# Attention units issued two at a time in a hybrid attention and recurrence layer

## The chip, the cores and the metric

One core of one Trainium2 chip runs the whole kernel. The metric is device time in microseconds (us), the median of a few runs. The program's engines are TensorE (PE, with PEld for its weight loads), VectorE (DVE), ScalarE (ACT), GpSimd (POOL) and the DMA queues, of which SyncE (SP) issues nearly all.

## What is computed

One inference step of one layer over 2048 prompt rows and 32 sample rows. Eight heads do stick-breaking attention, eight heads a matrix-state recurrence, and a projection and a gated feed-forward follow. The part that the change touches is the attention of the prompt:

```python
z = einsum('bqhd,bkhd->bhqk', q, k) / sqrt(64)
mask = k_pos < q_pos
log_1mb = where(mask, log_sigmoid(-z), 0)
after = reverse_cumsum(log_1mb) - log_1mb
weight = where(mask, exp(log_sigmoid(z) + after), 0)
o = einsum('bhqk,bkhd->bqhd', weight, v)
...
x = x + concat(attention, recurrence) @ w_out
x = x + (silu(h2 @ w_gate) * (h2 @ w_up)) @ w_down
```

## The kernel before

The kernel has three stages one after the other: the input projection (to about 940 us of the profile), the middle stage, and the output projection with the feed-forward. The middle stage is the one at issue. It has three generators, which one loop (L1165 to L1173) advances by turns, always the one with the least issued work for its size: `attention()` (L924), `recurrence()` (L997), which walks 33 chunks of 64 rows and each time goes from PE to DVE or ACT and back five times, and `first_rows()` (L1142), which does a part of the output projection.

`attention()` walks head by head through blocks of 512 queries (qg) and of 512 keys (kc), from the newest keys to the oldest. A block has four score units and four turn units. 

- A score unit, `scores` (L818), takes 128 queries: two matmuls (L824, L825, the high and the low part of an fp32 split) into a tile z in PSUM, on a diagonal block a third (L827) that adds the mask, then `stick` (L774): ACT makes the sigmoid R of z (L776) and DVE runs a multiplying scan over R, backwards (L778), which also reads z. Pool psZ has 3 buffers for z.
- A turn unit, `turn` (L832), takes 128 keys: up to four transposes (L837) of pieces of R into a tile wt in PSUM, then `split` (L103): ACT casts wt to wth (L104), and DVE subtracts wth from wt to get wtl (L105). Pool psW has 2 buffers for wt, so the transposes of a turn wait for the subtraction of the turn before the last.
- A values unit, `values` (L844), multiplies wth and wtl with the value rows (L851, L852) and sums in one PSUM tile (psO).

There are 320 units of each kind for the prompt, plus 6 for the sample rows (`s_scores`, `s_turn`, `s_values`). The main loop of `attention()` (L945 to L962) takes one unit of each per round: score unit t, then a turn whose last score lies LAG = 4 back, then the values of turns that are LAG2 = 2 rounds old. After that it yields to the other generators, with the work of the round as its weight. A list scheduler then orders the instructions of each engine, mostly as they were issued, and lets one go ahead of another that it takes to be waiting. Transposes (L837, L875, L990) and the recurrence's matmuls run on plain fp32; scores, values and the output projection (L760) on the one-pass type fp32r.

Of the kernel before, what the change touches and what calls it, by code (L numbers as in the profile page):

```python
# [52 lines left out]
def kernel(ctx: ExitStack, tc: tile.TileContext, x_prompt, x_sample, cache_k, cache_v,  # L53
# [709 lines left out]
    with tc.tile_pool(reuse_waits="tile", name="bp", bufs=6) as bp, \  # L763
# [8 lines left out]
        NB, LAG, LAG2, LOOK, RW = 12, 4, 2, 8, PAST + TS + 1  # L772
# [45 lines left out]
        def scores(h, qg, kc, j):  # L818

            k = pieces[h, kc][0]  # L820
            n = (j + 1) * P if kc == qg else 512
            z = psZ.tile([P, 512], F32, tag="z", name="z")
            js = slice(j * P, (j + 1) * P)
            PE.matmul(z[:, 0:n], state[h, qg][:, 0, js], k[:, 0:n], start=True, stop=False)  # L824
            PE.matmul(z[:, 0:n], state[h, qg][:, 1, js], k[:, 0:n], start=False, stop=kc != qg)  # L825
            if kc == qg:
                PE.matmul(z[:, n - P:n], identr, mnegr, start=False, stop=True)  # L827
            R = bk.tile([P, 512], F32, tag="R", name="R", bufs=NB)
            stick(z, R, n, 1.0 if kc == qg else state[h, qg, kc + 1, j][:, 0:1])
            state[h, qg, kc, j] = R  # L830

        def turn(h, qg, kc, kb):  # L832

            j0 = kb if kc == qg else 0
            pt = psW.tile([P, 512], F32, tag="wt", name="wt")
            for j in range(j0, 4):
                PE.transpose(pt[:, j * P:(j + 1) * P], state[h, qg, kc, j][:, kb * P:(kb + 1) * P], ident)  # L837
            wh = bq.tile([P, 512], F32R, tag="wth", name="wth", bufs=4)
            wl = bq.tile([P, 512], F32R, tag="wtl", name="wtl", bufs=4)
            c0 = j0 * P  # L840
            split(wh[:, c0:], wl[:, c0:], pt[:, c0:])
            state[h, qg, kc, "w", kb] = (wh, wl)
# [19 lines left out]
        def s_scores(kc, e):  # L862
            n = TS if kc == 2 else 512
            if kc == 2:
                R = bs.tile([P, RW], F32, tag="Rs", name="Rs")
                POOL.memset(R[:, PAST + TS:PAST + TS + 1], 1.0)
                state["R", e] = R
            elif e == 0:
                ck = bs.tile([P, TP], F32, tag="ck", name="ck").rearrange("p (j n) -> p j n", j=4)
                kT = bs.tile([P, TP], F32, tag="kT", name="kT").rearrange("p (c k) -> p c k", c=4)  # L870
                SP.dma_start(ck, cache_k[0, 0, kc * 512:(kc + 1) * 512].rearrange("(j p) h d -> p j (h d)", p=P))
                for c in range(4):
                    pt = psW.tile([P, 512], F32, tag="wt", name="ckt")
                    for j in range(4):
                        PE.transpose(pt[:, j * P:(j + 1) * P], ck[:, j, c * P:(c + 1) * P], ident)  # L875
                    (ACT.copy if c % 2 else DVE.tensor_copy)(kT[:, c, :], pt)
                SP.dma_start(ck, cache_v[0, 0, kc * 512:(kc + 1) * 512].rearrange("(j p) h d -> p j (h d)", p=P))
                state["ck", kc], state["kT", kc] = ck, kT
            z = psZ.tile([P, 512], F32, tag="z", name="zs")
            if kc == 2:  # L880
                PE.matmul(z[:, 0:n], ident, mnegs, start=True, stop=False)
            for c in range(4):
                rhs = kTs[64 * e:64 * e + 64, c, :] if kc == 2 else state["kT", kc][64 * e:64 * e + 64, c, :]
                PE.matmul(z[32 * c:32 * c + 32, 0:n], qTs[64 * e:64 * e + 64, c, :], rhs,
                          start=kc < 2, stop=True)
            b = bs.tile([P, 512], F32, tag="bs", name="bs", bufs=4)
            s_stick(z, state["R", e], b, kc * 512, n)
            state["b", kc, e] = b

        def s_turn(kc, e):  # L890
            n = TS if kc == 2 else 512
            pt = psW.tile([P, 512], F32, tag="wt", name="wts")
            for k0 in range(0, n, P):
                m = min(P, n)
                PE.transpose(pt[0:m, k0:k0 + P], state["b", kc, e][:, k0:k0 + m], ident)
            wT = bs.tile([P, 512], F32, tag="wTs", name="wTs")
            m = min(P, n)
            DVE.tensor_copy(wT[0:m, 0:max(n, P)], pt[0:m, 0:max(n, P)])
            state["w", kc, e] = wT

        def s_values(kc, e):
            n = TS if kc == 2 else 512
            if kc == 2 and e == 0:
                av = psO.tile([P, 512], F32, tag="av", name="avs")
                state["o"] = av
                PE.matmul(av[0:64, 0:H * TS], vTs[:, 0:HD], zr.to_broadcast([TS, H * TS]), start=True, stop=False)
            av, wT = state["o"], state["w", kc, e]
            for k0 in range(0, n, P):
                m = min(P, n)
                for c in range(4):  # L910
                    h = 2 * c + e
                    vv = vTs[:, h * HD:(h + 1) * HD] if kc == 2 else state["ck", kc][:, k0 // P, h * HD:(h + 1) * HD]
                    PE.matmul(av[0:64, h * TS:(h + 1) * TS], vv, wT[0:m, k0 + 32 * c:k0 + 32 * c + 32],
                              start=False, stop=kc == 0 and k0 == 384 and e == 1 and c == 3)
            if kc == 0 and e == 1:
                os_ = bq.tile([64, 512], F32, tag="oT", name="os", bufs=2)
                ACT.copy(os_[:, 0:256], av[0:64, 0:256])
                SP.dma_start(mixT_d[0:512, TP:TT].rearrange("(h d) q -> d h q", d=HD),
                             os_[:, 0:256].rearrange("d (h q) -> d h q", q=TS))
# [4 lines left out]
        def attention():  # L924
            A, B, loads = [], [], []
            for hq, h in [(hq, h) for hq in range(2) for h in range(H)]:
                if hq == 0 and h == 2:
                    for kc in (2, 1, 0):
                        for e in range(2):
                            A.append((lambda kc=kc, e=e: s_scores(kc, e), 1.0 if kc == 2 else 3.0))  # L930
                        for e in range(2):
                            B.append((len(A) - 1, lambda kc=kc, e=e: s_turn(kc, e),
                                      lambda kc=kc, e=e: s_values(kc, e), 0.2 if kc == 2 else 2.0))
                for qg in (2 * hq, 2 * hq + 1):
                    for kc in range(qg, -1, -1):
                        loads.append((len(A), h, qg, kc))
                        for j in range(4):
                            n = (j + 1) * P if kc == qg else 512
                            A.append((lambda h=h, qg=qg, kc=kc, j=j: scores(h, qg, kc, j), 2 * n / 2400))
                        for kb in range(4):  # L940
                            m = 4 - (kb if kc == qg else 0)
                            B.append((len(A) - 1, lambda h=h, qg=qg, kc=kc, kb=kb: turn(h, qg, kc, kb),
                                      lambda h=h, qg=qg, kc=kc, kb=kb: values(h, qg, kc, kb),
                                      m * (0.107 + 2 * P / 2400)))
            t, nb, pend = 0, 0, []  # L945
            while t < len(A) or nb < len(B) or pend:
                w = 0.0
                while loads and loads[0][0] <= t + LOOK:
                    load(*loads.pop(0)[1:])
                if t < len(A):  # L950
                    A[t][0]()
                    w += A[t][1]
                if nb < len(B) and (B[nb][0] <= t - LAG or t >= len(A)):
                    B[nb][1]()
                    pend.append((t, B[nb][2]))
                    w += B[nb][3]
                    nb += 1
                while pend and (pend[0][0] <= t - LAG2 or nb == len(B)):
                    pend.pop(0)[1]()
                    done["values"] += 1  # L960
                t += 1
                yield w  # L962

        def normalise(Yt, t0, n):

# [200 lines left out]
        while gens:  # L1166
            g = min(gens, key=lambda x: x[1] / x[2])
            with priority(tc, g[3]):
                w = next(g[0], None)
# [14 lines left out]
    with tc.tile_pool(reuse_waits="tile", name="c1", bufs=1) as cp, tc.tile_pool(reuse_waits="tile", name="psM", bufs=6, space=PSUM) as psM, \  # L1184
# [38 lines left out]
        with tc.tile_pool(reuse_waits="tile", name="co", bufs=2) as co:  # L1223
            gb = co.tile([P, D], F32, name="gb", bufs=1)
            SP.dma_start(gb, norm_ffn_g.to_broadcast([P, D]))
            wpool, w = done["w"]
            ws = wo_weights(co, 0, lambda: row2("wor"))
            w = next(ws), w
# [159 lines left out]
```

## Time and profile before

| | us |
|---|---|
| median of 3 runs | 3451.93 (3447.23 to 3460.93) |
| the profiled execution, its own time | 3450.89 |
| its span, first to last instruction | 3448.7 |
| PE busy in the span | 3273.3 (95%) |
| DVE busy in the span | 1763.8 (51%) |
| middle stage, first score to last values matmul | about 945 to 1785 |

The shares of busy time are means over three stages with different limits. The middle stage is the only one whose instructions move, so it has to be read by itself.

### The profile page before, as it was taken

What the parts mean: (1) busy time and instruction counts of PE and PEld (TensorE: products, weight loads), DVE (VectorE), ACT (ScalarE), POOL (GpSimd) and SP (SyncE); (2) the same over time, 40 slices, a digit from 0 to 9 for tenths busy, and PEclk for the clock granted to TensorE, in tenths of its full rate; (3) what the DMA queues carried; (4) which work ended last, traced back from release to release, by engine and by line L of the source; (5) the groups of instructions that cost most, each with busy time, mean ns of one, the idle gap of its engine ahead of it and who ended that gap; (6) DMA issues with size and microseconds to landing.
All of it is one profiled execution on the core that took longest, in us unless ns stands there. A gap on an engine that the chain in (4) does not pass through costs nothing.

```text
span 3448.7 us, 50501 instructions
## 1 busy us (share of the span) xinstructions
PE 3273.3 (95%) x20281; PEld 2830.4 (82%) x20281; DVE 1763.8 (51%) x2449; ACT 1159.5 (34%) x2231; POOL 856.4 (25%) x719
## 2 busy tenths in 40 slices
PE   8998898889699999999999999999999999999998
PEld 7988898878567777777777999999999888888887
DVE  4675757678679788887762322222222323212223
ACT  6434353434256455555542411111112311111111
POOL 3322423253101121122123421122112321222121
PEclk9999999989899899999999999999999999999999
DMA  5555564565765665656544511111111411111111
GB/s 149 162 157 153 174 175 137 172 181 153 209 178 149 157 152 156 171 143 159 158 106 128 192 50 45 42 50 43 43 49 56 166 49 42 50 43 49 49 43 49
DMA packets 481762, 395.82 MB, mean 115 GB/s; under 512 B 72228, under 2 KB 403568, under 8 KB 481528
## 3 DMA queue, kind: packets, MB, share of 16 engines
q1 hardware_dynamic: 393000, 346.58, 35.2%
q10 hardware_dynamic: 88528, 46.02, 5.0%
q8 instruction: 160, 2.62, 0.3%
q14 instruction: 74, 0.61, 0.1%
HBM read 278.19 MB, written 114.31 MB: 114 GB/s over the span
## 4 chain that ended last, share of the span: by engine, by line
PE 50%; DVE 1%; DMA 1%; issue 0%; ACT 0%; POOL 0%; SPq 0%; POOLq 0%; ACTq 0%
PE gu L1301 29%; PE dn L1321 15%; PE mo L760 3%; PE wt L837 0%; PE pt L1217 0%; DVE R L778 0%; PE av L851 0%; PE av L852 0%; DMA mx<-mixT_d 0%; PE z L825 0%; PE sap L1100 0%; PE yp L1122 0%; PE snp L1109 0%; PE yp L1124 0%; PE z L824 0%
## 5 line engine op out<-in xcount | busy, mean ns | idle before, releaser
L1324 DVE TENSOR_TENSOR x<-x,dn 128x512 f32<-128x512 f32 x374 | 255.7, 687 | 243.3 <-PE dn L1321 243.3
L778 DVE TENSOR_TENSOR_SCAN R<-R,z 128x512 f32<-128x512 f32 (+2 forms) x320 | 347.7, 1089 | 57.8 <-ACT R L776 55.0
L1301 PE MATMUL gu<-h2h,wh 128*128 128x352 f32 (+1 forms) x1760 | 368.3, 351 | 1.7 <-ACT wh L104 1.2
L1301 PE MATMUL gu<-h2h,wl 128*128 128x352 f32 (+1 forms) x1760 | 369.0, 351 | 0.0
L1301 PE MATMUL gu<-h2l,wh 128*128 128x352 f32 (+1 forms) x1760 | 367.3, 351 | 0.0
L1301 PEld LDWEIGHTS gu<-h2h,wh 128*128 128x128 f32 x1760 | 305.0, 188 | 33.9 <-ACT wh L104 1.4
L1301 PEld LDWEIGHTS gu<-h2l,wh 128*128 128x128 f32 x1760 | 305.3, 188 | 31.0
L1301 PEld LDWEIGHTS gu<-h2h,wl 128*128 128x128 f32 x1760 | 305.1, 188 | 30.2
L1321 PE MATMUL dn<-dh,hdh 128*128 128x512 f32 x748 | 295.1, 394 | 0.0
L1321 PE MATMUL dn<-dh,hdl 128*128 128x512 f32 x748 | 295.0, 394 | 0.0
L1321 PE MATMUL dn<-dl,hdh 128*128 128x512 f32 x748 | 293.8, 393 | 0.0
L324 PE MATMUL mm<-hh,wh 128*128 128x384 f32 (+4 forms) x1296 | 248.8, 334 | 2.7 <-ACT xp L336 1.2
L324 PE MATMUL mm<-hh,wl 128*128 128x384 f32 (+4 forms) x1296 | 235.6, 324 | 0.0
L324 PE MATMUL mm<-hl,wh 128*128 128x384 f32 (+4 forms) x1296 | 231.3, 320 | 0.0
L776 ACT ACTIVATE R<-z 128x512 f32<-128x512 f32 (+2 forms) x320 | 171.2, 537 | 151.0 <-PE z L825 82.5
L324 PEld LDWEIGHTS mm<-hh,wh 128*128 128x128 f32 (+1 forms) x1296 | 211.7, 193 | 9.8 <-ACT xp L336 1.6
L324 PEld LDWEIGHTS mm<-hh,wl 128*128 128x128 f32 (+1 forms) x1296 | 212.0, 191 | 2.6
L324 PEld LDWEIGHTS mm<-hl,wh 128*128 128x128 f32 (+1 forms) x1296 | 207.5, 187 | 2.6
L105 DVE TENSOR_TENSOR wtl<-wt,wth 128x512 fp32r<-128x512 f32 (+1 forms) x320 | 189.0, 591 | 27.0 <-ACT wth L104 25.5
L837 PE MATMUL wt<-ident,R 128*128 128x128 f32 x1088 | 186.2, 283 | 14.2 <-DVE wtl L105 13.6
L104 ACT CAST wth<-wt 128x512 fp32r<-128x512 f32 (+1 forms) x320 | 166.6, 521 | 80.7 <-PE wt L837 77.1
L104 ACT CAST dh<-rawd 128x1024 fp32r<-128x1024 f32 x44 | 44.2, 1049 | 426.8 <-PE dn L1321 424.4
(754 smaller groups left out, 5459.9 us busy)
## 6 DMA issues: line engine op xcount, KB each, us to landing
wraw<-in_w_in ACTq DMA_DIRECT2D x77, 512.0 KB
rawg<-in_w_gate SPq DMA_DIRECT2D x44, 512.0 KB
rawu<-in_w_up SPq DMA_DIRECT2D x44, 512.0 KB
rawd<-in_w_down SPq DMA_DIRECT2D x44, 512.0 KB
A_d<-a SPq DMA_DIRECT2D x28, 512.0 KB
mx<-mixT_d SPq DMA_DIRECT2D x27, 512.0 KB
k<-khl_d SPq DMA_DIRECT2D x42, 256.0 KB
vp<-vhl_d SPq DMA_DIRECT2D x42, 256.0 KB
```

Source lines behind the costliest of these rows:

```text
L104: ACT.copy(hi, src)
L105: (eng or DVE).tensor_tensor(lo, src, f32(hi), ALU.subtract)
L324: PE.matmul(ps[0:wd, 0:s1 - s0], a_[:, kt, 0:wd], b_[:, kt, s0:s1], start=i == 0, stop=i == 3 * KT - 1)
L760: PE.matmul(ps[0:n], a_[:, kt, 0:n], b_[:, kt, :], start=j + kt == 0, stop=j == 2 and kt == KT - 1)
L776: ACT.activation(R[:, 0:n], z[:, 0:n], AF.Sigmoid, scale=-0.125)
L778: DVE.tensor_tensor_scan(rv, rv, z[:, 0:n], before, ALU.mult, ALU.bypass)
L837: PE.transpose(pt[:, j * P:(j + 1) * P], state[h, qg, kc, j][:, kb * P:(kb + 1) * P], ident)
L1301: PE.matmul(ps[:, 0:n], a_[:, kt, :], b_[:, kt, s0:s1], start=i == 0, stop=i == 23)
L1321: PE.matmul(ps[0:n], a_[:, i * P:i * P + n], b_[:, ds_], start=k == 0, stop=k == 3 * len(js) - 1)
L1324: DVE.tensor_tensor(x1[:n, ds_], x1[:n, ds_], ps[0:n], ALU.add)
```

## The change

The main loop of `attention()` is rewritten. A round now issues two score units, then up to two turn units, yields to the other generators with half of the round's weight, issues the two values units that belong to the turns of the round before, and yields again. LAG still sets how far a turn stays behind its scores; LAG2 is no longer used. Nothing is computed differently, and no pool, tile or DMA is added or removed. Lines after L968 move down by 4.

```diff
             t, nb, pend = 0, 0, []
             while t < len(A) or nb < len(B) or pend:
                 w = 0.0
                 while loads and loads[0][0] <= t + LOOK:
                     load(*loads.pop(0)[1:])
-                if t < len(A):
-                    A[t][0]()
-                    w += A[t][1]
-                if nb < len(B) and (B[nb][0] <= t - LAG or t >= len(A)):
-                    B[nb][1]()
-                    pend.append((t, B[nb][2]))
-                    w += B[nb][3]
-                    nb += 1
-                while pend and (pend[0][0] <= t - LAG2 or nb == len(B)):
-                    pend.pop(0)[1]()
+                for i in range(t, min(t + 2, len(A))):
+                    A[i][0]()
+                    w += A[i][1]
+                ready, pend = pend[:2], pend[2:]
+                for _ in range(2):
+                    if nb < len(B) and (B[nb][0] <= t + 1 - LAG or t >= len(A)):
+                        B[nb][1]()
+                        pend.append(B[nb][2])
+                        w += B[nb][3]
+                        nb += 1
+                yield w / 2
+                for fn in ready:
+                    fn()
                     done["values"] += 1
-                t += 1
-                yield w
+                t += 2
+                yield w / 2
```

What it does to the order shows on two engines. The first place is PE in the middle of the attention, around a diagonal block. Before, one unit of each kind follows the other:

```order
L824 MATMUL z<-k,q 128x256
L825 MATMUL z<-k,q 128x256
L827 MATMUL z<-mnegr,identr 128x128
L837 MATMUL wt<-ident,R 128x128 x4
L851 MATMUL av<-wth,vp 128x512
L852 MATMUL av<-wtl,vp 128x512
L824 MATMUL z<-k,q 128x384
```

With the change, the same scores stand there (the first row belongs to the round's first unit):

```order
L824 MATMUL z<-k,q 128x128
L825 MATMUL z<-k,q 128x128
L827 MATMUL z<-mnegr,identr 128x128
L824 MATMUL z<-k,q 128x256
L825 MATMUL z<-k,q 128x256
L827 MATMUL z<-mnegr,identr 128x128
L837 MATMUL wt<-ident,R 128x128 x8
L1094 MATMUL up<-VST,QAc 64x64 x8
L851 MATMUL av<-wth,vp 128x512
L852 MATMUL av<-wtl,vp 128x512
```

Two scores, eight transposes in a row, a piece of the recurrence (L1094, which was L1090), and then the values of the round before, of which a second pair follows the last row. PE changes from fp32 to fp32r work once per two units here, not once per unit.

The second place is DVE at the same scores. Before (R names the scan, wtl the subtraction; the numbers are those of the tiles):

```order
L1092 COPY Us_14646<-up_14637 64x512 [waits PE_49]
L778 SCALAR_TENSOR_TENSOR R_14652<-R_14652,z_14648 128x256 [waits Activation_49]
L105 TENSOR_TENSOR wtl_14661<-wt_14655,wth_14660 128x512 [waits Activation_49]
L778 SCALAR_TENSOR_TENSOR R_14670<-R_14670,z_14666 128x384 [waits Activation_49]
L105 TENSOR_TENSOR wtl_14679<-wt_14673,wth_14678 128x512 [waits Activation_49]
```

With the change:

```order
L778 SCALAR_TENSOR_TENSOR R_14634<-R_14634,z_14630 128x128 [waits Activation_49]
L778 SCALAR_TENSOR_TENSOR R_14641<-R_14641,z_14637 128x256 [waits Activation_49]
L105 TENSOR_TENSOR wtl_14650<-wt_14644,wth_14649 128x512 [waits Activation_49]
L105 TENSOR_TENSOR wtl_14659<-wt_14653,wth_14658 128x512 [waits Activation_49]
L1096 COPY Us_14671<-up_14662 64x512 [waits PE_49]
```

Scan and subtraction alternated (L1092, now L1096, is a copy of the recurrence); now two scans stand ahead of two subtractions.

## Rows read from the trace of the kernel before

**Rows 1.** The page, part 1: busy us (share of the span) xinstructions.
```profile
PE 3273.3 (95%) x20281; PEld 2830.4 (82%) x20281; DVE 1763.8 (51%) x2449; ACT 1159.5 (34%) x2231; POOL 856.4 (25%) x719
```

**Rows 2.** Windows: stretch, length, busy us per engine (xcount), granted clock, DMA share, GB/s.
```profile
945.00:1300.00 355.00, 328.94 (x2818) 260.92 (x2818) 293.43 (x407) 197.40 (x444) 49.44 (x47) 0.95 0.62 160
1300.00:1785.00 485.00, 472.46 (x4010) 378.65 (x4010) 383.65 (x493) 250.32 (x493) 99.72 (x78) 1.00 0.57 151
```

**Rows 3.** Timeline of PE: start us, us, engine, line, operation, count.
```profile
1307.56 0.47 PE L851 MATMUL av<-wth,vp 128*128 128x512 f32 x1
1307.87 0.39 PE L852 MATMUL av<-wtl,vp 128*128 128x512 f32 x1
1308.10 0.34 PE L824 MATMUL z<-k,q 128*128 128x384 f32 x1
...
1308.52 0.60 PE L837 MATMUL wt<-ident,R 128*128 128x128 f32 x4
1308.87 0.48 PE L851 MATMUL av<-wth,vp 128*128 128x512 f32 x1
1309.19 0.40 PE L852 MATMUL av<-wtl,vp 128*128 128x512 f32 x1
```

**Rows 4.** Timeline, weight loads (PEld) of the same two values matmuls.
```profile
1308.85 0.19 PEld L851 LDWEIGHTS av<-wth,vp 128*128 128x128 f32 x1
...
1308.95 0.19 PEld L852 LDWEIGHTS av<-wtl,vp 128*128 128x128 f32 x1
```

**Rows 5.** Waits of PEld, 945 to 1785 us: us in total, times, longest us.
```profile
PEld wt L837 <- DVE wtl L105: 30.6, 60, 2.4
PEld z L824 <- DVE R L778: 18.1, 27, 1.9
...
PEld sap L1100 <- DVE M L1048: 4.5, 10, 1.2
```

**Rows 6.** Waits of PE itself, the same stretch (not contained in rows 5).
```profile
PE wt L837 <- DVE wtl L105: 13.6, 27, 2.0
PE z L824 <- DVE R L778: 9.7, 16, 1.7
```

**Rows 7.** Waits of PEld, then of PE, 1300 to 1790 us.
```profile
PEld wt L837 <- DVE wtl L105: 11.3, 20, 2.4
...
PEld z L824 <- DVE R L778: 4.4, 7, 1.3
PE wt L837 <- DVE wtl L105: 4.7, 11, 2.0
...
PE z L824 <- DVE R L778: 1.5, 2, 1.0
```

**Rows 8.** Groups by line on DVE, 940 to 1800: xcount, busy us, mean ns, idle before.
```profile
L778 DVE TENSOR_TENSOR_SCAN R<-R,z 128x512 f32<-128x512 f32 (+2 forms) x320 | 347.7, 1089 | 57.8 <-ACT R L776 55.0
L105 DVE TENSOR_TENSOR wtl<-wt,wth 128x512 fp32r<-128x512 f32 (+1 forms) x320 | 189.0, 591 | 27.0 <-ACT wth L104 25.5
```

**Rows 9.** Windows with lowered granted clock, columns as in rows 2.
```profile
1125.00:1185.00 60.00, 51.72 (x436) 41.05 (x435) 42.72 (x61) 28.93 (x65) 5.44 (x6) 0.91 0.69 177
1185.00:1245.00 60.00, 59.73 (x525) 49.69 (x524) 52.51 (x69) 31.02 (x63) 10.39 (x11) 0.91 0.57 137
...
1605.00:1665.00 60.00, 57.17 (x456) 44.77 (x455) 46.99 (x63) 29.52 (x58) 14.68 (x12) 0.97 0.56 149
```

## The prediction

> **What bounds the kernel now.** The page's shares come first [rows 1]: PE is busy for 95% of the span and DVE for 51%. That mean hides the middle stage, so the windows of that stage come next [rows 2]. From 945 to 1300 us PE is busy for 328.9 of 355 us (93%) and DVE for 293.4 (83%). From 1300 to 1785 PE has 472.5 of 485 (97%), DVE 383.7 (79%). So PE sets the pace, with DVE close behind, and closer in the first part. The waits say who makes PE stop [rows 5, 6]: transposes (L837) wait for the subtraction that frees their PSUM buffer, 30.6 + 13.6 = 44.2 us in 87 waits, and scores (L824) wait for the scan that frees z, 18.1 + 9.7 = 27.8 us in 43 waits. All other waits on one cause are far smaller; the largest row behind these, of the recurrence, is 4.5 us. Of the 72.0 us that PE loses to DVE, 11.3 + 4.4 + 4.7 + 1.5 = 21.9 us lie after 1300 [rows 7], the other 50.1 before. The first 355 us are thus a stretch in which DVE often sets the pace, the later 485 us one in which PE does.
>
> **The change part by part.** It removes and adds no instruction. It moves them, on PE, ACT and DVE. The loads stay: units come in fours and sixes, so every load falls on an even unit and goes out at the same one as before, and SP's and POOL's queues keep their order to within a unit. The other generators get the same weight, in two portions.
>
> *Fewer changes of type on PE: a gain.* In the timeline [rows 3] the values matmul L852, which follows another fp32r matmul, has the next start 1308.10 - 1307.87 = 0.23 us later. L851, of the same 512 columns but right behind transposes, takes 1309.19 - 1308.87 = 0.32 us, and 1307.87 - 1307.56 = 0.31 the other time. Entering fp32r work from fp32 work costs 0.09 us. Leaving it costs nothing that shows: the four transposes at 1308.52 take 0.35 us, as many as four take without a change ahead. I counted the entries in PE's order from the first score to the last values matmul: 478 before, 350 with the change. 128 x 0.09 = 11.5 us of PE time. In the later stretch it is on the path, since PE sets the pace there. In the first, 355 of 840 us, a shorter PE partly only waits longer for DVE. With entries spread evenly, 11.5 x 355 / 840 = 4.9 us belong there; I count half. The gain taken is 9.1 us, with 6.6 and 11.5 as its bounds.
>
> The Trainium skill, page "TensorE: Matmul & The Clock Gate", Part 2, "Step-by-step: what each phase is for", says that TensorE pulls a weight load ahead of matmuls in flight, so that the next weights load while this matmul runs. By that rule alone an entry would cost nothing, and the gain would be 0. The trace differs at just this place [rows 4]: the load of L852 starts 0.24 us ahead of its matmul (1308.95 against 1309.19), that of L851 behind transposes only 0.02 us ahead (1308.85 against 1308.87). So the measured 0.09 us stands.
>
> *Transposes in pairs: a loss.* psW has two buffers, and a pair of turns needs both. Before, a subtraction stood behind one scan on DVE; now the first subtraction of a pair stands behind two. A scan takes 1.089 us on average [rows 8]. Against that, the second score of the pair is also run ahead of the transposes on PE, and this moves the transposes themselves later by about 0.41 us: two matmuls of 0.23 at 512 columns, the mean width being 435, plus the mask now and then. So the buffer is freed 1.09 - 0.41 = 0.68 us later relative to the transposes. What stands between one use of a buffer and the next on PE (two values, two scores, one turn and what the other generators put in) is as much as before. A pair pays if it was waiting anyway: 87 of 320 turns waited, 27%, so 43 of 160 pairs, 43 x 0.68 = 29.6 us. From below the cost is 0, if other work of the generators fills the time; from above 160 x 0.68 = 109 us, if every pair waits. Of the waits, 20 + 11 = 31 of 87 lie after 1300 [rows 7]: their part, 10.5 us, counts in full. The part before 1300, 19.1 us, I halve for the same reason as the gain: where DVE sets the pace, the order of scans and subtractions changes nothing in its sum of work. Together 20.1 us. Behind the waiting transposes stand the values of the round before and the next scores, which need not wait themselves; they are late with it, as PE takes its matmuls in order.
>
> *Scores in pairs: a small gain.* z has three buffers. The first score of a pair now reuses one that was filled two rounds ago and will rarely wait; only the second needs the scan of the last round. If the first scores' share went, it would be half of 27.8 us, 13.9. But such waits come where the diagonal blocks make the turns short and several scores stand in a row, and these places remain. Bounds 0 and 13.9; I take 4.
>
> *The recurrence.* Its copies on DVE may now stand behind two scans. The largest such wait is 4.5 us in all [rows 5], so doubling it costs 4.5 and halving it saves 2.3; I take 0, since five crossings per chunk fall anywhere in a round.
>
> *The clock.* The granted clock is 0.91 in two windows of 60 us and 0.97 in another [rows 9], after stretches in which PE mostly had the recurrence's small matmuls and waits. Of the two levels, 1.2 and 2.4 GHz, the lower then held for about (0.09 + 0.09 + 0.03) x 2 x 60 = 25 us, which costs about half of it, 12.6 us. It may fall elsewhere and more or less often with the new order. I take no change, and +-10 us for the range.
>
> Sum: -9.1 + 20.1 - 4.0 = +7.0 us. Against the profiled execution's own 3450.9 us (the span of 3448.7 and 2.2 around it) this gives 3457.9; I say **3458 us**. That execution stands 1 us below the median of the runs, 3451.9.
>
> **The rivals.** *Slower: the pairs wait.* psW as a pair of buffers that is filled and emptied at once: each of the 43 pairs pays 0.68 us in full, in the first stretch too, and its second turn also waits, since its subtraction comes 0.59 us [rows 8] after the first's while the first turn's transposes fill only 0.35. That is 43 x (0.68 + 0.24) = 39.6, less 11.5, so +28 us: 3479. It decides from 29 us of added waits on, where the sum passes 0.5%. For it: 87 waits now, on a subtraction that will come later. Against it: most waits lie where DVE sets the pace anyway.
>
> *Faster: only the saving counts.* The added waits stay out, because two portions of other work now stand between a pair and the next, and the first scores' waits go: -11.5 - 13.9 = -25 us, 3425. For it: PE at 97% after 1300 with little wait. Against it: nothing in the change makes a subtraction come earlier.
>
> *Weight loads are hidden.* No gain from fewer entries, losses as in the forecast: 20.1 - 4.0 = +16, 3467. The rule named above would give this; rows 3 and 4 speak against it.
>
> *The change doesn't do what it says.* The scheduler could undo the pairs. The order shows them on both engines, and 128 entries fewer; but it has the transposes ahead of the older values, where the change's title has them last. If the pairs made no difference to PE: 3451.
>
> **How the numbers follow.** A measurement of this kernel tells about 0.5%, 17 us, from no change, so "same" is 3435 to 3469. Chances: forecast 0.50, slower rival 0.26, faster rival 0.18, hidden loads 0.04, no effect 0.02. The forecast's own bounds, with the clock's 10 us, put 0.06 of its 0.50 over 3469 and 0.01 under 3435; most of the slower rival (0.22) and most of the faster (0.17) lie beyond the lines, and of the hidden loads 0.02. Faster 0.18, slower 0.30, same 0.52. The range runs from 3430, a little above the faster rival, to 3486, the slower rival with part of the clock's 10 us; about 1 in 10 is left out at either end.
>
> **What would show it.** Right: L851's and L824's starts in a pair lie 0.23 us from the next where they now lie 0.32; transposes waiting for L105 rise from 44.2 to some 65 us, with the number of waits falling toward half but each longer; scores waiting for L778 fall slightly from 27.8; the feed-forward after 1905 us keeps its length. Wrong: waits for L105 that stay at 44 or fall (then the faster rival), or go past 84 (the slower one); an entry into fp32r that costs less in long runs; a change outside of the middle stage; or lowered clock in stretches that now run at 1.00.

## The result and the profile after

The changed kernel takes 3437.03 us, the median of six runs (3431.45 to 3441.31), against 3451.76 (3447.23 to 3460.93) for the kernel before, six runs. The ratio on record is 0.9943, 95% interval [0.9922, 0.9964], which is 12 to 27 us faster; the two medians stand 14.7 us apart, the two profiled executions 19.4. The forecast was 3458 us, a small loss. The medians of E1 and E2 below take in one slow run each of twelve, which the ratios and the means leave out; without it they are 3466.2 and 3447.3 us. The profiled execution took 3431.45 us with a span of 3429.6, 19.1 less than before.

Part 1 of the page of the changed kernel answers to [rows 1], and its two windows of the middle stage (stretch, length, busy us per engine, granted clock, DMA share, GB/s) to [rows 2]:

```profile
PE 3258.3 (95%) x20281; PEld 2829.6 (83%) x20281; DVE 1752.8 (51%) x2449; ACT 1151.4 (34%) x2231; POOL 861.8 (25%) x719
```

```profile
945.00:1300.00 355.00, 326.12 (x2890) 264.55 (x2889) 294.79 (x414) 199.30 (x450) 53.96 (x49) 0.97 0.63 162
1300.00:1785.00 485.00, 474.48 (x4007) 385.01 (x4006) 377.35 (x494) 245.00 (x494) 102.89 (x79) 1.00 0.57 151
```

The shares have hardly moved. What moved is how far the work has got: 2890 matmuls instead of 2818 up to 1300 us, at a granted clock of 0.97 instead of 0.95. In the trace the attention, from its first score to its last values, is 13.1 us shorter (839.8 to 826.7 us), and the first feed-forward matmul starts 20.3 us earlier (1911.5 to 1891.2). From there to the end both kernels need the same (1537 and 1538 us).

Next the waits of PEld and of PE from 945 to 1785 us (total, times, longest), which answer to [rows 5, 6]:

```profile
PEld wt L837 <- DVE wtl L105: 21.2, 41, 1.3
PEld z L824 <- DVE R L778: 15.2, 28, 1.1
```

```profile
PE wt L837 <- DVE wtl L105: 9.3, 15, 1.2
PE z L824 <- DVE R L778: 6.7, 17, 0.8
```

The transposes wait less (21.2 us against 30.6), in fewer waits (41 against 60), the longest 1.3 us against 2.4. The scores wait slightly less (15.2 against 18.1). The forecast had the first row rise by half.

These rows also show a misreading ahead of the prediction. [Rows 6] were called "not contained in rows 5". They are contained: in the trace of before, 27 of PE's 27 waits for L105 and 15 of its 16 for L778 end with a wait of PEld for the same tile. A weight load that waits makes its matmul wait, and both are listed. The two waits for DVE are 30.6 + 18.1 = 48.7 us, not 72.0. With the change they are 21.2 + 15.2 = 36.4, so 12.3 us less. Not all of that is lost time, since the matmul ahead can still run while a weight load waits: PE itself stood idle for 13.6 + 9.7 = 23.3 us of it before and for 9.3 + 6.7 = 16.0 with the change.

These two rows aren't all. The waits of PEld for anything, from the first score to the first feed-forward matmul, add up to 148.4 us in the trace of before and to 128.3 with the change. This sum will explain more than the two rows do.

The two costs on DVE that the prediction used stay as they were [rows 8], in the groups by line, 940 to 1800 us:

```profile
L778 DVE TENSOR_TENSOR_SCAN R<-R,z 128x512 f32<-128x512 f32 (+2 forms) x320 | 338.5, 1084 | 73.3 <-ACT R L776 70.8
L105 DVE TENSOR_TENSOR wtl<-wt,wth 128x512 fp32r<-128x512 f32 (+1 forms) x320 | 178.9, 595 | 15.5 <-ACT wth L104 14.2
```

The last change is the clock. The same three windows as in [rows 9]:

```profile
1125.00:1185.00 60.00, 53.35 (x484) 43.13 (x483) 49.29 (x73) 32.81 (x77) 6.20 (x9) 0.97 0.65 169
1185.00:1245.00 60.00, 55.71 (x502) 44.68 (x501) 53.09 (x70) 35.92 (x73) 14.79 (x11) 1.00 0.64 167
1605.00:1665.00 60.00, 59.78 (x520) 48.99 (x520) 46.35 (x63) 29.67 (x63) 14.58 (x12) 1.00 0.53 135
```

0.91, 0.91 and 0.97 have become 0.97, 1.00 and 1.00. Over the span the mean granted clock is 0.979 against 0.976, so (1 - 0.976) x 3448.7 = 83 us were lost to the lower level before and 72 after (0.001 of the clock, its last place, is 3.4 us). A way to keep the two causes apart is the **time at full clock**: the time less (1 - mean granted clock) x span. It is a reckoning, which takes all of that loss to be on the path. It holds up well: the 23 runs of before that stand beside E1 to E4 scatter by 7.4 us (standard deviation) in time, but by 3.2 in time at full clock. The table after the experiments uses it for every kernel.

### The profile page after: what moved, and what is told of

Read it like the earlier page. It is cut to its first block, busy times and chain, and to the rows that moved or that the text cites. A ratio compares the mean times of both kernels' runs of the same rounds, so it can differ in the third digit from the quotient of the medians.

```text
span 3429.6 us, 50515 instructions
## 1 busy us (share of the span) xinstructions
PE 3258.3 (95%) x20281; PEld 2829.6 (83%) x20281; DVE 1752.8 (51%) x2449; ACT 1151.4 (34%) x2231; POOL 861.8 (25%) x719
## 4 chain that ended last, share of the span: by engine, by line
PE 50%; DVE 1%; DMA 0%; ACT 0%; issue 0%; POOL 0%; POOLq 0%; ACTq 0%; SPq 0%; DVEq 0%
PE gu L1305 29%; PE dn L1325 15%; PE mo L760 3%; PE wt L837 0%; PE pt L1221 0%; PE av L851 0%; PE av L852 0%; DVE R L778 0%; PE z L824 0%; PE sap L1104 0%; PE z L825 0%; PE snp L1113 0%; DMA mx<-mixT_d 0%; ACT yt L1213 0%; PE yp L1126 0%
## 5 line engine op out<-in xcount | busy, mean ns | idle before, releaser
L778 DVE TENSOR_TENSOR_SCAN R<-R,z 128x512 f32<-128x512 f32 (+2 forms) x320 | 338.5, 1084 | 73.3 <-ACT R L776 70.8
L776 ACT ACTIVATE R<-z 128x512 f32<-128x512 f32 (+2 forms) x320 | 163.5, 535 | 159.0 <-PE z L825 98.2
L104 ACT CAST dh<-rawd 128x1024 fp32r<-128x1024 f32 x44 | 44.2, 1047 | 425.4 <-PE dn L1325 424.4
L105 DVE TENSOR_TENSOR wtl<-wt,wth 128x512 fp32r<-128x512 f32 (+1 forms) x320 | 178.9, 595 | 15.5 <-ACT wth L104 14.2
L104 ACT CAST wth<-wt 128x512 fp32r<-128x512 f32 (+1 forms) x320 | 156.0, 529 | 53.4 <-PE wt L837 51.1
L837 PE MATMUL wt<-ident,R 128*128 128x128 f32 x1088 | 162.6, 278 | 10.2 <-DVE wtl L105 9.3
```

Source lines behind the costliest of these rows:

```text
L104: ACT.copy(hi, src)
L105: (eng or DVE).tensor_tensor(lo, src, f32(hi), ALU.subtract)
L776: ACT.activation(R[:, 0:n], z[:, 0:n], AF.Sigmoid, scale=-0.125)
L778: DVE.tensor_tensor_scan(rv, rv, z[:, 0:n], before, ALU.mult, ALU.bypass)
```

## The experiments

### Half of the change: E1 and E2

E1 pairs the scores alone: two scores in a row, then turn, values, turn, values. E2 pairs the turns and values alone. Both yielded twice per round, as the change does. E1's round:

```diff
+                for i in range(t, min(t + 2, len(A))):
+                    A[i][0]()
+                    w += A[i][1]
+                ready, pend = pend[:2], pend[2:]
+                for n in range(2):
...
+                        w += B[nb][3]
...
+                    if not n:
+                        yield w / 2
+                    if ready:
+                        ready.pop(0)()
...
+                t += 2
+                yield w / 2
```

> Only the scores go in pairs (score, score, turn, values, turn, values); VectorE's two scans stand together as in the change, while PE enters one-pass work from fp32 work 440 times (478 before, 350 with the change). Theory A (the gain is the saved entries at 0.09 us each, pairing the scans costs nothing): 38 entries fewer, 3.4 us below the kernel before, some 3448 us. Theory B (the prediction's: pairing the scans delays the subtraction and costs about 20 us, and something else paid for it): 10 to 20 us above the kernel before, 3462 to 3472. Theory C (waiting on VectorE fell because the scores go in pairs, and that is most of the gain): close to the changed kernel, 3437 to 3442.

> Turns and values go in pairs, the scores singly (score, turn, turn, score, values, values). Entries 325, 25 fewer than with the change; the scans stand apart on VectorE. Theory A: 153 x 0.09 = 13.8 us below the kernel before, about 3438, like the change. Theory B: better than the change by the 20 us that the paired scans cost, about 3418. Theory C (pairs of scores matter): little gain, 3445 to 3452.

E1 took 3466.38 us, ratio 1.0022 [1.0006, 1.0037]; E2 3448.66, 0.9961 [0.9945, 0.9977]. Neither is a clean half. At the first `yield w / 2` the second turn (in E2 the second score) isn't in `w` yet, so a round reports less than it issued, and the loop, which advances the generator with the least reported work, lets the attention run ahead. In E1 the last values come at 1704 us and the recurrence ends at 1805. What is left alone then runs badly. The window of 1700 to 1810 us, of the changed kernel and of E1:

```profile
1700.00:1810.00 110.00, 105.58 (x763) 85.21 (x763) 63.59 (x84) 46.65 (x87) 34.85 (x20) 0.98 0.48 135
```

```profile
1700.00:1810.00 110.00, 95.42 (x794) 78.37 (x793) 30.70 (x46) 20.05 (x34) 27.14 (x22) 0.75 0.47 123
```

With DVE busy for 31 us instead of 64 and PE for 95 instead of 106, the granted clock is 0.75 in E1. Its mean clock is the lowest of all kernels, 0.968, though its time at full clock (3355) is as good as the change's. E2 has the lowest time at full clock of all kernels, 3345, and loses it again to its clock, 0.9705. The two runs tell what the balance between the generators is worth, not what the halves are worth.

### The halves with the right weight: E5 and E6

The same orders; the first yield now reports what has been issued, the second the rest:

```diff
+                w0 = w
+                yield w0
...
+                yield w - w0
```

> E1 again, but with the weight that attention reports to the other generators equal to its work, so that attention, recurrence and output projection end together again as before (in E1 attention ended 100 us ahead of the recurrence). Scores in pairs, turn and values alternating; 438 entries. Theory A (only entries count): 40 x 0.09 = 3.6 us below the kernel before, ratio 0.999. Theory B (paired scans cost some 20 us): 16 us above, ratio 1.005. Theory C (paired scores cut the waiting): ratio 0.996 or less.

> E2 again with the weight mended: turn and values in pairs, scores apart, 351 entries, as many as with the change (350). Theory A: 127 x 0.09 = 11.4 us below the kernel before, ratio 0.9967, little above the change's 0.9943. Theory B (paired scans cost): clearly below the change, ratio 0.990. Theory C (paired scores are what helps): ratio 0.999 or more.

E5 (scores in pairs) took 3437.9 us, 0.9951 [0.9934, 0.9968]. That is the whole gain, with 438 entries into fp32r work, nearly the 478 of before. E6 (turns in pairs) took 3452.1, 0.9989 [0.997, 1.0008], no gain that can be measured, with 351 entries, as few as the change. So the number of entries doesn't decide. The waits of PEld, 945 to 1785 us, first of E5, then of E6:

```profile
PEld wt L837 <- DVE wtl L105: 27.0, 42, 1.6
PEld z L824 <- DVE R L778: 14.0, 21, 2.4
```

```profile
PEld z L824 <- DVE R L778: 24.6, 32, 2.3
PEld wt L837 <- DVE wtl L105: 15.4, 40, 1.1
```

Pairing an operation shortens the waits in its own place: scores in pairs 18.1 to 14.0 (and the transposes' 30.6 to 27.0), turns in pairs 30.6 to 15.4 while those of the scores go from 18.1 to 24.6. In sum both lie near 40 us, 8 to 9 less than before. At full clock both are also 9 to 10 us better than before (3356.6 and 3355.7 against 3365.6). What parts them is the clock: E5's runs have 0.9762, E6's 0.9716.

### What an entry costs: E7 and E8

E7 puts one small fp32 matmul (32 columns, its result overwritten) between two scores, where PE stays on fp32r otherwise. E8 puts the same matmul ahead of the transposes of every second turn, where PE is on fp32 anyway. So E7 adds 160 matmuls and, as counted in PE's order, 477 - 350 = 127 entries; E8 the matmuls alone (330 entries).

```diff
+            if j % 2:
+                PE.matmul(z[:, 0:TS], ident, mnegs, start=True, stop=True)
             PE.matmul(z[:, 0:n], state[h, qg][:, 0, js], k[:, 0:n], start=True, stop=False)
```

> The changed kernel with one small fp32 matmul (32 columns, its result is overwritten) ahead of every second score, between two one-pass matmuls: 160 more fp32 pieces, entries 477 against 350. With E8 it prices an entry on the path: theory A, E7 stands 147 x 0.09 = 13 us above E8. If PE's waits take the entries up, E7 and E8 are alike.

> The same 160 small fp32 matmuls, but ahead of the transposes of every second turn, so beside fp32 work: 330 entries. Each costs PE one weight load and 32 columns, so 160 x 0.06 to 0.1 = 10 to 16 us above the changed kernel if PE's time counts in full, less if it falls into waits.

E7 took 3453.99 us (0.9994 [0.9979, 1.0008]), E8 3449.94 (0.9986 [0.9974, 0.9998]). PE's timeline (start, us, engine, line, operation), first of E7, where L825 is the added matmul (one such product is two instructions on PE, in one row) and L826 and L827 are the score's two; then of E8, where L837 is the added one and L839 the transposes:

```profile
1405.86 0.39 PE L827 MATMUL z<-k,q 128*128 128x512 f32 x1
1406.09 0.30 PE L825 MATMUL z<-mnegs,ident 128*128 128x32 f32 x2
1406.22 0.48 PE L826 MATMUL z<-k,q 128*128 128x512 f32 x1
1406.54 0.39 PE L827 MATMUL z<-k,q 128*128 128x512 f32 x1
```

```profile
1399.84 0.62 PE L839 MATMUL wt<-ident,R 128*128 128x128 f32 x4
1400.30 0.31 PE L837 MATMUL wt<-mnegs,ident 128*128 128x32 f32 x2
1400.44 0.63 PE L839 MATMUL wt<-ident,R 128*128 128x128 f32 x4
```

In E7 the added matmul takes 0.13 us (1406.09 to 1406.22), and the score behind it 0.32 to the next start instead of 0.23 (1405.86 to 1406.09). So it costs PE 0.22 us, 35 us in all. In E8 it takes 0.14 us (1400.30 to 1400.44), and the first transpose behind it takes 0.144 us where a transpose behind another takes 0.109 (medians over the trace): 0.18 us, 28 in all. Of the 0.09 us that the score pays behind the added matmul, a plain fp32 transpose thus pays 0.035 as well; not more than 0.05 can be the entry into fp32r. Against the changed kernel the times at full clock rise by 13 and 11 us only. Meanwhile the waits shrink: those for L105 and L778 from 36.4 us to 21.3 in E7 (10.8 and 6.6, and 3.9 at the added matmul) and 30.6 in E8 (14.9 and 13.3, and 2.4 at the added matmul), and all waits of PEld from 128.3 to 104.3 and 106.9. Between E7 and E8 lie 477 - 330 = 147 entries, some 7 us of PE's time, and 2 +-3 us of time at full clock. Work that is added to PE comes back in part as shorter waits.

### One yield, and the values first: E3 and E4

E3 yields once per round, after the turns. E4 issues the older values first, then scores and turns, then yields once:

```diff
                 ready, pend = pend[:2], pend[2:]
+                for fn in ready:
+                    fn()
...
-                yield w / 2
-                for fn in ready:
-                    fn()
...
                 t += 2
-                yield w / 2
+                yield w
```

> The change with one yield per round, right behind the two turns, so that other generators' fp32 work follows the transposes. Entries 338 against 350. Theory A: 1 us below the change, not to be told from it, 3436. If the second yield is what spreads other work between the pairs and so keeps transposes from waiting: waits of transposes on the subtraction go up from 30 us, and the time by some 5 to 15 us.

> The order that the change's title names: two scores, then the two older values, then the two turns, one yield. Entries 349 against 350. Theory A: as the change, 3437 within 4 us. If the place of the values between scores and transposes gives VectorE time for the scans, transposes wait less than 30 us for the subtraction and it is some 5 us faster; the values may instead wait for the subtraction of the round before.

E3 took 3438.62 us (0.993 [0.9908, 0.9952]), as the change: where the other generators' work is put in between matters little. E4 took 3434.43 (0.9922 [0.9903, 0.9941]). Its waits of PEld:

```profile
PEld z L824 <- DVE R L778: 21.4, 28, 3.2
PEld av L852 <- DVE wtl L105: 17.6, 35, 2.1
...
PEld av L851 <- ACT wth L104: 7.4, 15, 1.8
```

The transposes no longer wait for the subtraction at all. The values, which now stand right behind the recurrence's work, wait in their place, for the same subtraction. The sum of these three rows, 46.4 us, is larger than the change's two, yet the time at full clock is 4 us shorter (+-4). All waits of PEld together do fall, from 128.3 to 122.1 us. So a few rows of waits can mislead where an edit moves waits to other rows.

### A third buffer for the transposes: E9 and E10

To keep the number of PSUM buffers, a third one for wt takes one from z. E9 does this to the kernel before, E10 to the change.

```diff
-            tc.tile_pool(reuse_waits="tile", name="psZ", bufs=3, space=PSUM) as psZ, \
-            tc.tile_pool(reuse_waits="tile", name="psW", bufs=2, space=PSUM) as psW, \
+            tc.tile_pool(reuse_waits="tile", name="psZ", bufs=2, space=PSUM) as psZ, \
+            tc.tile_pool(reuse_waits="tile", name="psW", bufs=3, space=PSUM) as psW, \
```

> The kernel before with three buffers for the transposes (psW) and two for the scores (psZ) instead of two and three. Theory D (since E5 to E8): the change saves PE no work that counts, it makes PE wait less on VectorE, and less waiting also keeps the clock up. Then transposes' waits on the subtraction fall from 44 us toward 0; scores' waits on the scan rise from 28 us. If it is the buffers alone, the sum of the two waits moves with the time: a sum near 50 us gives some 3440, a sum above 72 more than 3452. Theory A (entries into one-pass work): no change of entries, 3452 whatever the waits do.

> The changed kernel with psW 3 and psZ 2. A pair of scores then fills both buffers of z, so the first score of a pair waits for the first scan of the pair before: theory D: scores' waits rise from 22 us to 60 or more, transposes' fall below 15, and the time is 10 to 30 us above the change's. Theory A: 3437.

E9 took 3452.96 us (0.9991 [0.9977, 1.0006]), E10 3437.53 (0.9936 [0.9922, 0.995]). The loss that was expected of E10, whose pairs of scores would find both buffers of z in use, did not come in its time. The waits of PEld, of E9, then of E10:

```profile
PEld z L824 <- DVE R L778: 39.1, 58, 2.2
...
PEld wt L837 <- DVE wtl L105: 3.2, 5, 1.7
```

```profile
PEld z L824 <- DVE R L778: 46.4, 69, 2.3
...
PEld wt L837 <- DVE wtl L105: 3.4, 13, 0.3
```

The waits change their place: the pool with the fewest buffers decides where PE waits. The sum of the two rows goes from 48.7 to 42.3 us in E9, and the time stays, where a sum near 50 was expected to give some 3440 us. In E10 it goes from 36.4 to 49.8, above the kernel before, and the time stays again. At full clock E10 does lose 5 us against the change (3361 against 3356), but its clock, 0.9778, is the highest of all with that of E12 and gives 5 us back. So these two rows of waits by themselves don't make the change's gain.

### Less work on DVE: E11 and E12

E11 is the change with one multiplication of the recurrence's normalisation (L986, which was L982; 0.69 us, 16 of 17 of them) on GpSimd. E12 is the same edit on E4.

```diff
-            DVE.tensor_tensor(y3, y3, st[0:n, 1].unsqueeze(2).to_broadcast([n, H, HD]), ALU.mult)
+            (DVE if t0 == TP - P else POOL).tensor_tensor(y3, y3, st[0:n, 1].unsqueeze(2).to_broadcast([n, H, HD]), ALU.mult)
```

> The changed kernel with one multiplication per 128 rows of the normalisation (L982, 17 of 0.9 us, 15 us in all) moved from VectorE to GpSimd. Theory D: waits on VectorE fall from 52 us by some 5 to 10 us, and the time with them, to about 3430. If VectorE's load doesn't set the waits: as the change, 3437.

> E4 (two scores, two values, two turns, one yield) with the same multiplication on GpSimd, the combination that could beat both kernels: 3428 to 3434 if both gains hold, 3434 if E4's is all.

E11 took 3432.91 us (0.9927 [0.991, 0.9943]), E12 3426.69 (0.9903 [0.9887, 0.9919]), the fastest of all. 16 x 0.69 = 11 us less on DVE lowers the median by 4 us against the change and by 8 against E4; the intervals of each pair overlap, so the part of this edit alone isn't certain. E12's interval lies wholly below that of the change: it beats both kernels, before by 1%, the change by 10 us.

### Pairs of scores early or late: E13 and E14

After E1 to E12, time at full clock and clock had come apart, but why the clock is higher was open. In the profiles of before, E6 and E9 (single scores) the granted clock of 1060 to 1300 us is 0.96, 0.93 and 0.95; in those with pairs of scores and the right weight it is 0.97 to 0.99, but for E8, which has 0.94. E13 pairs the scores for the first 130 units only (to about 1240 us), E14 from there on only; turns and values are single in both.

```diff
+                two = t < 130
+                for i in range(t, min(t + 1 + two, len(A))):
+                    A[i][0]()
+                    w += A[i][1]
```

> Scores are issued in pairs for the first 130 units (to about 1240 us of the span), singly after it; turns and values stay single throughout. In the profiles so far the granted clock of 1060 to 1300 us is 0.93 to 0.96 where scores are single and 0.97 to 0.99 where they are paired, and 1785 to 1915 us has 0.96 to 0.97 against 0.97 to 1.00. Theory (the pairs hold the clock up in the early stretch, where DVE often sets the pace): that stretch at 0.97 or above here, a mean clock of about 0.975 to 0.977 in the runs, some 80 to 88 us lost to it, and a median of 3438 to 3446. Rival one (what counts is how the attention ends): the early stretch as in the kernel before, mean clock 0.973, median about 3450. Rival two (an accident of each order): the two runs of this pair do not differ in mean clock by more than 0.001.

> The complement: scores single for the first 130 units, in pairs after it. Theory: 1060 to 1300 us at 0.93 to 0.96 as in the kernel before, mean clock 0.972 to 0.974, some 90 to 97 us lost to it, median 3446 to 3456, and so 5 to 12 us above the early pairs. Rival one (the end of the attention counts): 1785 to 1915 us at 0.99, mean clock 0.976, median about 3440, below the early pairs. Rival two: no difference in mean clock over 0.001 between the two.

E13 took 3441.16 us (0.9964 [0.9947, 0.998]), E14 3452.14 (0.9989 [0.9973, 1.0005]). At full clock the two are alike, 3358.6 and 3359.7 (each has part of the gain), but the mean clock of twelve runs each is 0.9757 against 0.9732. The 23 runs of before beside them have 0.9741, the standard errors are 0.0005 to 0.0007. So the early pairs go with a higher clock, as the theory had it, and the late ones don't; but E13 is only 0.0016 above before, where E5 is 0.0029 above the runs beside it. The place isn't confirmed by the profiles. Windows of 1060 to 1300 us of before, of the change, of E13, of E14, and of E8, which has pairs of scores throughout:

```profile
1060.00:1300.00 240.00, 224.00 (x1946) 178.87 (x1945) 201.92 (x274) 134.51 (x293) 39.14 (x35) 0.96 0.60 152
```

```profile
1060.00:1300.00 240.00, 224.04 (x2029) 181.29 (x2028) 203.56 (x281) 137.02 (x299) 42.96 (x37) 0.99 0.60 156
```

```profile
1060.00:1300.00 240.00, 226.57 (x1955) 182.11 (x1956) 197.68 (x272) 134.79 (x291) 39.11 (x35) 0.94 0.58 154
```

```profile
1060.00:1300.00 240.00, 224.78 (x1983) 180.73 (x1980) 199.56 (x279) 135.84 (x299) 39.98 (x35) 0.96 0.62 158
```

```profile
1060.00:1300.00 240.00, 229.45 (x2041) 191.27 (x2040) 197.99 (x271) 132.45 (x293) 39.58 (x35) 0.94 0.58 149
```

The profiled execution of E13 has 0.94 in just the stretch where 0.97 or more was expected. It took 3447.9 us at a mean clock of 0.974, below the 0.9757 of its runs, so it may be one of its poorer executions; E8's took 3456.6 us, above its median too. One profile per kernel can't settle it.

### All kernels by their clock

Means over the runs that the ratios use (two standard errors behind the +-). Lost is (1 - clock) x span. Entries are of the order; "two rows" are the waits of PEld for L105 and L778, 945 to 1785 us (of E4 and E12 those for L104 too), "all waits" those of PEld for anything from the first score to the first feed-forward matmul, both of the one profiled execution. The runs of before beside E5 to E14 have times at full clock of 3365 to 3366.

| kernel | entries | two rows, us | all waits, us | clock | lost, us | time at full clock |
|---|---|---|---|---|---|---|
| before (23 runs beside E1 to E4) | 478 | 48.7 | 148.4 | 0.9735 | 92 | 3367 +-1 |
| the change | 350 | 36.4 | 128.3 | 0.9763 | 81 | 3356 +-2 |
| E1 scores in pairs, weight too small | 440 | 37.9 | 140.8 | 0.9678 | 111 | 3355 +-2 |
| E2 turns in pairs, weight too small | 325 | 29.0 | 124.0 | 0.9705 | 102 | 3345 +-2 |
| E3 one yield | 338 | 38.0 | 127.0 | 0.9762 | 82 | 3356 +-2 |
| E4 values first | 349 | 46.4 | 122.1 | 0.9760 | 82 | 3352 +-3 |
| E5 scores in pairs | 438 | 41.0 | 132.3 | 0.9762 | 82 | 3357 +-2 |
| E6 turns in pairs | 351 | 40.0 | 129.9 | 0.9716 | 98 | 3356 +-2 |
| E7 added matmuls, with entries | 477 | 21.3 | 104.3 | 0.9750 | 86 | 3369 +-2 |
| E8 added matmuls, no entries | 330 | 30.6 | 106.9 | 0.9758 | 83 | 3367 +-2 |
| E9 before, 3 buffers wt, 2 z | 473 | 42.3 | 139.2 | 0.9731 | 93 | 3363 +-2 |
| E10 the change, 3 and 2 | 367 | 49.8 | 133.2 | 0.9778 | 76 | 3361 +-2 |
| E11 the change, less on DVE | 351 | 39.8 | 127.4 | 0.9767 | 80 | 3354 +-2 |
| E12 values first, less on DVE | 344 | 36.3 | 119.1 | 0.9778 | 76 | 3350 +-2 |
| E13 pairs of scores early | 463 | 40.4 | 139.7 | 0.9757 | 84 | 3359 +-2 |
| E14 pairs of scores late | 457 | 39.2 | 135.6 | 0.9732 | 93 | 3360 +-1 |

Against these 23 runs the change's gain is half time at full clock (3367 to 3356, 11 us) and half clock (92 to 81, 11 us). The six runs of before that stand beside the change itself have a median 4.5 us lower than the 23, and their clocks aren't on record, so there the clock's part may be smaller.

The first half has its explanation in the table. Leave out E1 and E2, whose weights don't add up, and E7 and E8, which add work to PE. Over the other twelve kernels, which give PE the same matmuls, the time at full clock follows the sum of all waits with a correlation of 0.96, at 0.56 us for each us of waiting; the change's 20.1 us less waiting would make 11 us of it. With the two rows alone the correlation is 0.55. The entries have 0.77, since kernels with fewer entries mostly wait less too. Where entries and waits part, the time goes with the waits: E5 with 438 entries and E6 with 351 wait alike (132.3 and 129.9 us) and stand at 3357 and 3356, and E9, with about the entries of before (473), waits less (139.2) and stands at 3363. For the second half the table shows only that the clock is at or above 0.9757 in every kernel that pairs the scores from the start with the right weight and leaves PE's work alone, and at or below 0.9741 in those with single scores at the start, the runs of before beside each experiment included.

## Why the prediction was wrong

The result lies inside the range, but on the other side of no change than the forecast. By its steps:

**Fewer changes of type on PE, -9.1 us: the size was misread.** The 0.09 us between L851 behind transposes and L852 was there, but it is paid back one slot earlier. PE's timeline of the changed kernel has a run of eight transposes:

```profile
1387.25 1.03 PE L837 MATMUL wt<-ident,R 128*128 128x128 f32 x8
1388.04 0.48 PE L851 MATMUL av<-wth,vp 128*128 128x512 f32 x1
1388.36 0.39 PE L852 MATMUL av<-wtl,vp 128*128 128x512 f32 x1
1388.59 0.40 PE L851 MATMUL av<-wth,vp 128*128 128x512 f32 x1
```

Eight transposes take 1388.04 - 1387.25 = 0.79 us to the start of L851; the four of [rows 3] take 0.35. So four more cost 0.44, 0.11 each, and four alone at that price would take 0.44, not 0.35. The last slot of a run is short by the same 0.09 us by which the next is long. From the first transpose to the second values matmul a unit alone takes 0.67 us [rows 3], a pair 1.11 and then one further fp32r slot, 0.23: twice 0.67 is 1.34, and 1.11 + 0.23 is 1.34 too. Averaged over all such places in both traces the saved entry is worth 0.005 us at most. The prediction compared the four transposes only with other runs of four, all with the same short slot. The Trainium skill, page "TensorE: Matmul & The Clock Gate", Part 2, "Step-by-step: what each phase is for", says that the next weights load while a matmul runs, from which the prediction took that an entry costs nothing. Behind transposes the two traces agree with that (0.005 us at most), and the start of L851's load [rows 4], by which the prediction set it aside, did not bear on the price. Behind 32-column fp32 matmuls E7 shows 0.09 us on PE, of which at most 0.05 is the entry.

Nor would a real saving on PE have counted in full: the prediction counted half of it up to 1300 us and all of it later, but E7 and E8 added 35 and 28 us to PE and the time at full clock rose by 13 and 11.

**Transposes in pairs, +20.1 us: the step that set the sign, and it failed.** Its 43 waiting pairs came from the 87 waits that counted 27 twice. And the 0.68 us per pair isn't there: from the end of a turn's transposes to the end of its subtraction the mean over the turns of each trace is 2.75 us before and 2.87 after, 0.12 more. The subtraction starts 1.31 us after its cast before and 1.43 with the change. Between the two, the first subtraction of a pair meets 0.9 scans on average before and 1.4 with the change, where the forecast had one and two; the second meets 1.1 both times. So the order of DVE was read as a time. Against the small delay stands what the prediction named but didn't price: a pair that waits mostly waits once, and the second turn finds its buffer free. Before, the first turns of pairs waited 33 times for L105 (19.2 us) and the second ones 27 times (11.4 us); with the change it is 30 times (18.3 us) and 11 times (2.8 us). Nearly all of the fall from 30.6 to 21.2 us is in the second turns. The step took a rise of the transposes' waits where they fell by 9.4 us.

**Scores in pairs, -4 us.** 18.1 to 15.2 us, -2.9: right in sign and near in size. E5, where nothing else is paired, has -4.1.

**The recurrence, 0.** The 4.5 us that the prediction called its largest wait became 3.2. A larger row that [rows 5] leave out, 10.9 us of L1046 for which the profile shows no cause, became 11.6. Neither speaks against 0.

**The clock, 0 +-10.** The term was set at the wrong place, with bounds that were about right: 72 us lost in the profiled execution against 83, so -11, and 11 in the means. E5 against E6 and E13 against E14 tie it to pairs of scores, the latter to those of the first 130 units, though the profiles of E13 and E8 don't show it there. By what these keep the clock up is open. That PE stops more briefly in that stretch would fit (in the profile of before the clock is 0.83 from 1130 to 1140 us and 0.74 from 1140 to 1150, around waits of PE of 1.7 us for L778 and 1.5 for L105), but E6 has shorter waits of the transposes and the lowest clock of the kernels with the right weight, and E10 has the longest waits of the scores, 46.4 us, and the highest clock.

In sum, of the span's -19.1 us, -11 are the clock, and the 8 that are left are near the 11 that 20.1 us less waiting of PEld come to at 0.56 us each; the waits for L105 and L778 are 12.3 of these 20.1. That the waits are the cause of the time at full clock is argued from the order of twelve kernels: the edit that comes nearest to moving waits alone is E9's, with 9 us less of them and 3 +-2 less at full clock than the runs of before beside it. The rival "only the saving counts" (3425) had the sign, but its -11.5 for entries doesn't exist, and the scores' waits did not go. The rival with hidden weight loads (3467) was right on the entries and shared the false loss. The slower rival fell with its first term. That the range took in 3437 is owed to the rivals and the clock's 10 us, not to the forecast's steps.

## What to carry to other kernels

Price a change of type, or any switch, from the first instruction of the run before it to the second one behind it, and on runs of two lengths: a slot that looks long may be paid for by the one ahead. When two engines share the bound, count each wait once, compare the sum of all waits and not two rows of it, and expect work saved on one of them to come back in part as its wait for the other; a delay read from the order of a queue counts only if the instruction wasn't standing there already. Compare times with the granted clock of each run taken out before explaining 10 us of them, and when a generator is split into more yields, check that their weights add up to what it issued.

## What was not expected of the hardware

- The last of a run of transposes before an fp32r matmul has a slot of 0.35 - 3 x 0.11 = 0.02 us in the records, and the matmul behind it 0.32 instead of 0.23.
- Run times of one kernel follow its granted clock nearly one to one: the runs of before beside E1 to E4 go from 3446.5 us at 0.977 to 3469.8 at 0.971, 23 us, and 0.006 x 3450 is 21.
- A small change of order in the attention moves the mean clock between 0.968 (E1) and 0.978 (E10, E12), worth 35 us, as much as any edit here did to the work.
